# Moving the token sums of an up-projection from GpSimd to VectorE, asking later for two column sums, and moving one sum of a down-projection

## The chip, the cores and the metric

The kernel runs on one core of one Trainium2 chip. The metric is the device time of one execution in microseconds (us), as the median of several executions. A core has five engines with an instruction queue each: TensorE (PE, the matmuls), VectorE (DVE), ScalarE (ACT), GpSimd (POOL) and SyncE (SP), which here issues all the DMAs. Each engine takes the instructions of its queue in order; semaphores make an instruction wait for those of other engines.

## The reference, cut to what matters

One encoder block on 2048 tokens of width 1024, in float32: a mixer (a short convolution beside a gated linear attention), cross-attention into 256 memory rows, and a squared-ReLU MLP with a hidden width of 4096.

```python
def reference(x, mem, ...):
    for l in range(DEPTH):
        x = x + mixer_layer(x, ...)
        x = x + memory_cross_attention(x, mem, xa_norm[l], mem_norm[l], w_xq[l], w_xkv[l], w_xo[l])
        x = x + sq_relu_mlp(x, mlp_norm[l], w_up[l], w_down[l])
    return rms_norm(x, final_norm)

def sq_relu_mlp(x, mlp_norm, w_up, w_down):
    h = rms_norm(x, mlp_norm) @ w_up
    return jnp.square(jax.nn.relu(h)) @ w_down
```

The change touches the seam between the cross-attention and the MLP, the MLP's first product (up-projection) and its second (down-projection).

## The kernel before

**Precision and products.** Every float32 operand of a matmul is split into a high part (a cast on ACT, L113, in `split`) and a low part (a subtraction on DVE, L114), and a product is three matmuls: high by high, high by low, low by high (`mm3`, L141 to L143, or `product`, L1009). Activations lie transposed, features on the 128 partitions and tokens along the free axis.

**Order.** The program is written in Python, and a planner, which costs every instruction and orders each engine's queue by program order and by when it expects the operands, places the instructions. In the stretch of the change no engine's order is written by hand. A tile is taken from a ring of buffers with a fixed number (for instance seven `t2`, 28 `a`, eight `g`, two `st`, three `raw`, three `cv`, and four `ps` and four `pg` banks of PSUM) and given back when its last reader is done.

**Cross-attention.** It goes over eight blocks of 256 tokens (`s` = 0 to 7, L1028). For a block, `xa_probs` (L703) transposes the probabilities on PE (L712) and splits them, and `xa_out` (L717) multiplies them with the memory's values and adds the residual on DVE (L726). The last block uses `xa_last` (L729) instead: all eight PSUM banks are open at once, 192 matmuls run without a break, and eight additions on DVE (L741) empty them. After each block `sumsq` (L643) squares the result on ACT (L646, L648) and adds the squares up on DVE (L647, L649, L650, L651) to one 128x256 tile. `rstd_col` (L152) turns this tile into column sums by tiny matmuls with a vector of ones (L157), a scaling on DVE (L147) and a power on POOL (L149); `x2_rstd` (L654) stores the result in `rcol` (L657). In the last block `x2_rstd(s - 1)`, for block 6, stands between `xa_probs` and `xa_last`; block 7's own sum is asked for at L1063, before the loops of the up-projection, and stored at L1064. `x2_rows` (L659) spreads the values of `rcol` over the partitions, two blocks at a time. The values of blocks 6 and 7 are used first by `x2_rows` in the 13th step (`f == 12`) of the up-projection's first half.

**Up-projection.** It is a Strassen-like product with seven block products for eight. It runs over two halves of the tokens (`hf`, L1066) and in each over 16 steps (`f`, L1070). A step uses seven weight operands, made anew for each step by `weight_side` (L982) from `w_up`, and seven token operands, made once for each half by `token_side` (L960). Four 512-token by 512-feature quarters of the activations, loaded from `x2d` and scaled in `quarter` (L956, on DVE), are combined by `both` (L943): four calls in each half, for a22 + a21, that minus a11, a11 - a21, and a12 minus the second sum. Each call is two instructions of 128x1024. In the kernel before they run on POOL, through the helper `add` (L924). `operand` (L930) splits each result for the matmuls. The operands are used in the order 1, 4, 5, 6, 2, 7, 3. One step is 84 matmuls of 512 columns. ACT and DVE empty the banks: DVE's additions (L924) and squares (L1018), ACT's L1013, L1014 and L1084. The results go to `zu` in DRAM.

**Down-projection.** The same seven products over four groups of hidden features (`GROUPS`, of 4, 4, 3 and 3 blocks of 128), with the tokens in two parts, c = 0 and 1. `token_operands` (L1126) loads pieces of `zu` and combines them. `combine` (L1139) takes POOL unless it is told otherwise. It is called for s = u21 + u22 (POOL), for s - u11 (POOL), for a12 - s (DVE) and for a11 - a21 (POOL). `weight_operands` (L1162) does the like for the weights, on POOL. The matmuls are L1240, and DVE adds each bank into an accumulator (L924, `a<-ps,a` and `a<-pg,a`).

Of the kernel before, what the change touches and what calls it, by code (L numbers as in the profile page):

```python
# [30 lines left out]
def block_kernel(ctx, tc, x, mem, wm, wv, wlg, wlog, wout, wxk, wxv, wxqT, wxo, wup, wdn,  # L31
# [891 lines left out]
    def add(out, a, b, op=ALU.add, eng=nc.vector):  # L923
        eng.tensor_tensor(out=out, in0=a, in1=b, op=op)  # L924
# [17 lines left out]

    def both(out, a, b, op):  # L943
        for i in range(2):
            add(out[i], a[i], b[i], op, nc.gpsimd)

    def quarter(hf, b, k, t):

# [79 lines left out]
    for s in range(NS):  # L1028
        if s + 1 < NS:
            xa_scores(s + 1, 0, 0)  # L1030
            if s > 0:
                xa_probs(s, 0)
            xa_scores(s + 1, 0, 1)
            if s > 0:
                xa_probs(s, 1)
                x2_rstd(s - 1)
            xa_scores(s + 1, 1, 0)
            xa_scores(s + 1, 1, 1)
            if s == 0:
                xa_probs(s, 0)  # L1040
                xa_probs(s, 1)
        else:
            xa_probs(s, 0)
            xa_probs(s, 1)
            x2_rstd(s - 1)
            sides = [token_side(0)]
            next(sides[0])
            X = dict([next(sides[0])])
            W = weight_side(0, T2)
            X.update([next(sides[0])])  # L1050
            xa_last(s)
            f_last = sumsq(live[s]["xs"])
            continue
        xa_out(s, 0)
        if s + 2 < NS:
            xa_in(s + 2)
        if s in (4, 5):
            x2_rows(s - 4, s - 4)
        xa_out(s, 1)
        live[s]["f2"] = sumsq(live[s]["xs"])  # L1060
        if s + 2 < NS:
            xa_rstd(s + 2)
    r7 = rstd_col(f_last, PG)  # L1063
    nc.vector.tensor_copy(rcol[:, 14:16], r7)  # L1064

    for hf in range(2):  # L1066
        b0, b1 = 2 * hf, 2 * hf + 1
        if hf == 1:
            X = {}
        for f in range(16):  # L1070
            def x(i):
                if i not in X:
                    k, X[k] = next(sides[hf])
                    assert k == i
                return X[i]
            if f + 1 < 16:
                nxt = weight_side(f + 1)
            if hf == 0 and f == 14:
                sides.append(token_side(1))
                next(sides[1])  # L1080
            px, py, pz, pw = PS(), PG(), PS(), PG()
            product(px, W[1], x(1), True)
            c1 = T2()
            nc.scalar.copy(c1, px)  # L1084
            product(pw, W[4], x(4), True)
            product(pz, W[5], x(5), True)
            product(py, W[6], x(6), True)
            u2 = T2()
            add(u2, py, c1)
            product(px, W[2], x(2), False)  # L1090
            c11 = T2()
            sq_relu(c11, px, f, b0)
            product(py, W[7], x(7), False)
            add(c1, py, c1)
            c22 = T2()
            add(c22, pz, c1)
            sq_relu(c22, c22, f + 16, b1)
            add(c1, c1, pw, ALU.subtract)
            sq_relu_v(c1, f, b1)
            product(pz, W[3], x(3), False)  # L1100
            add(u2, pz, u2)
            sq_relu_v(u2, f + 16, b0)
            if hf == 0 and f == 12:
                for i in range(2):
                    x2_rows(2 + i, i)
            if hf == 0 and f == 15:
                nxt = weight_side(0)
            W = nxt
# [17 lines left out]
    def token_operands(c, fa, fb, n):  # L1126

        b0, b1 = 2 * c, 2 * c + 1

        def parts(src):  # L1130
            res = []
            for t in src:
                m = t.shape[1]
                hi, lo = (A4(F32R, (P, 2, TB))[:, :m] for _ in range(2))
                split(t, hi, lo)
                res += [(hi[:, j], lo[:, j]) for j in range(m)]
            return res

        def combine(out, a, b, op, eng=nc.gpsimd):  # L1139
            for o, x, y in zip(out, a, b):  # L1140
                add(o, x, y, op, eng)

        yield parts(raw_u(fa, n, b0))
        yield parts(raw_u(fb, n, b0))
        s = ST(F32, (P, 4, TB))
        s = [s[:, i:min(i + 2, n)] for i in range(0, n, 2)]
        for i, t in zip(range(0, n, 2), s):
            m = t.shape[1]
            nc.sync.dma_start(t, zu[(fa + i) * P:(fa + i + m) * P, b1 * TB:(b1 + 1) * TB].rearrange("(j p) t -> p j t", p=P))
        combine(s, s, raw_u(fb, n, b1), ALU.add)  # L1150
        yield parts(s)
        combine(s, s, raw_u(fa, n, b0), SUB)
        a12 = raw_u(fb, n, b0)
        combine(a12, a12, s, SUB, nc.vector)
        yield parts(a12)
        yield parts(s)
        yield parts(raw_u(fb, n, b1))
        a11 = raw_u(fa, n, b0)
        combine(a11, a11, raw_u(fa, n, b1), SUB)
        yield parts(a11)  # L1160
# [230 lines left out]
```

## Time and profile before

| | |
|---|---|
| median of 3 executions | 2741.66 us (2735.44 to 2743.51) |
| the profiled execution | 2743.17 us, with a span of 2741.3 us from its first to its last instruction |
| cross-attention's last block, from its transposes to the first up matmul | 1397.76 to 1431.16 us of the span |
| up-projection | 1431.16 to about 2078 us, its second half's matmuls from 1756.56 us |
| down-projection in seven products | about 2078 to 2610 us |

The page of the profile gives the share of each engine first, then the span in slices, the DMA queues, the chain of work that ended last, the costliest groups of instructions and the DMA issues. A row of the timeline reads: start, duration, engine, line, operation, output<-inputs, size, count, and in brackets how long the engine had sat idle and what ended it. Rows of one kind that follow each other are merged, with their count at the end. Several 128x1024 rows merged as x2 take twice the time of one.

### The profile page before, as it was taken

What the parts mean: (1) busy time and instruction counts of PE and PEld (TensorE: products, weight loads), DVE (VectorE), ACT (ScalarE), POOL (GpSimd) and SP (SyncE); (2) the same over time, 40 slices, a digit from 0 to 9 for tenths busy, and PEclk for the clock granted to TensorE, in tenths of its full rate; (3) what the DMA queues carried; (4) which work ended last, traced back from release to release, by engine and by line L of the source; (5) the groups of instructions that cost most, each with busy time, mean ns of one, the idle gap of its engine ahead of it and who ended that gap; (6) DMA issues with size and microseconds to landing.
All of it is one profiled execution on the core that took longest, in us unless ns stands there. A gap on an engine that the chain in (4) does not pass through costs nothing.

```text
span 2741.3 us, 34734 instructions
## 1 busy us (share of the span) xinstructions
PE 2611.3 (95%) x13560; PEld 2224.7 (81%) x13560; DVE 1632.1 (60%) x2430; ACT 933.6 (34%) x1432; POOL 396.7 (14%) x250
## 2 busy tenths in 40 slices
PE   7999989989889999999998999899999999999998
PEld 6898878877677787989886888688887788878877
DVE  6412363467757455343467557765655767788975
ACT  5411153423435443232234333433333222222322
POOL 1000010112210000000021000300002425243323
PEclk9999999999899999999999999999999999999999
DMA  7512355223444452101134332343338664545233
GB/s 246 180 61 68 100 175 167 77 89 116 129 122 157 150 184 85 62 31 47 47 119 151 104 119 96 112 139 115 113 117 301 203 200 143 178 160 183 94 104 112
DMA packets 198308, 353.26 MB, mean 129 GB/s; under 512 B 17344, under 2 KB 73792, under 8 KB 198144
## 3 DMA queue, kind: packets, MB, share of 16 engines
q1 hardware_dynamic: 198144, 351.05, 39.7%
q8 instruction: 106, 1.74, 0.3%
q14 instruction: 58, 0.48, 0.1%
HBM read 262.90 MB, written 88.08 MB: 128 GB/s over the span
## 4 chain that ended last, share of the span: by engine, by line
PE 76%; DVE 9%; DMA 5%; issue 4%; ACT 3%; POOL 2%; SPq 0%; POOLq 0%; DVEq 0%; ACTq 0%
PE ps L1009 12%; PE ps L141 9%; PE ps L142 9%; PE ps L143 9%; PE pg L1009 9%; PE pg L1240 8%; PE ps L1240 8%; PE pg L141 3%; PE pg L143 3%; PE pg L142 3%; DVE a L114 2%; DMA gt<-zv 1%; DVE g L114 1%; DMA raw<-zy 1%; DVE g L396 1%
## 5 line engine op out<-in xcount | busy, mean ns | idle before, releaser
L141 PE MATMUL ps<-a,a 128*128 128x512 f32 (+1 forms) x840 | 306.8, 365 | 6.8 <-DVE t L245 6.8
L142 PE MATMUL ps<-a,a 128*128 128x512 f32 (+1 forms) x840 | 306.2, 364 | 0.0
L143 PE MATMUL ps<-a,a 128*128 128x512 f32 (+1 forms) x840 | 306.1, 364 | 0.0
L1009 PE MATMUL pg<-a,g 128*128 128x512 f32 x1152 | 287.3, 395 | 13.1 <-DVE t L924 6.1
L1240 PE MATMUL pg<-a,g 128*128 128x512 f32 x1176 | 288.5, 392 | 10.4 <-DVE a L924 7.9
L1240 PE MATMUL ps<-a,g 128*128 128x512 f32 x1176 | 285.4, 389 | 1.7 <-DVE a L924 1.7
L1009 PE MATMUL ps<-a,g 128*128 128x512 f32 x1152 | 277.5, 389 | 0.2 <-ACT a L113 0.2
L1240 PEld LDWEIGHTS pg<-a,g 128*128 128x128 f32 x1176 | 222.6, 190 | 58.1 <-issue 8.9
L1009 PEld LDWEIGHTS pg<-a,g 128*128 128x128 f32 x1152 | 219.4, 191 | 61.5 <-DVE t L924 6.6
L1240 PEld LDWEIGHTS ps<-a,g 128*128 128x128 f32 x1176 | 220.7, 188 | 48.0 <-DVE a L924 2.1
L1009 PEld LDWEIGHTS ps<-a,g 128*128 128x128 f32 x1152 | 216.0, 188 | 45.4 <-ACT a L113 0.6
L113 ACT CAST a<-raw 128x1024 fp32r<-128x1024 f32 (+1 forms) x126 | 127.7, 1021 | 363.4 <-PE ps L1240 122.0
L114 DVE TENSOR_TENSOR a<-raw,a 128x1024 fp32r<-128x1024 f32 (+1 forms) x126 | 158.5, 1264 | 119.8 <-ACT a L113 118.0
L113 ACT CAST g<-gt 128x512 fp32r<-128x512 f32 x180 | 103.6, 618 | 342.9 <-PE pg L1009 203.8
L141 PEld LDWEIGHTS ps<-a,a 128*128 128x128 f32 x840 | 162.3, 193 | 32.4 <-DVE t L245 4.8
L143 PEld LDWEIGHTS ps<-a,a 128*128 128x128 f32 x840 | 162.7, 194 | 23.2
L142 PEld LDWEIGHTS ps<-a,a 128*128 128x128 f32 x840 | 162.5, 193 | 23.4 <-issue 0.2
L149 POOL TENSOR_TENSOR sm<-sm,nhalf 128x2 f32<-128x2 f32 (+1 forms) x26 | 23.0, 886 | 924.0 <-DVE sm L147 924.0
L114 DVE TENSOR_TENSOR g<-gt,g 128x512 fp32r<-128x512 f32 x180 | 142.5, 830 | 8.4 <-ACT g L113 8.3
L924 DVE TENSOR_TENSOR t<-pg,t 128x512 f32<-128x512 f32 x64 | 44.0, 688 | 172.6 <-PE pg L1009 170.7
L924 POOL TENSOR_TENSOR gt<-gt,t 128x512 f32<-128x512 f32 x42 | 65.7, 1581 | 459.7 <-DMA t<-in_wdn 390.1
L114 DVE TENSOR_TENSOR g<-raw,g 128x1024 fp32r<-128x1024 f32 (+3 forms) x90 | 103.3, 1158 | 33.0 <-ACT g L113 31.6
(327 smaller groups left out, 5380.8 us busy)
## 6 DMA issues: line engine op xcount, KB each, us to landing
zu<-t SPq DMA_DIRECT2D x128, 256.0 KB, 3.2
raw<-zu SPq DMA_DIRECT2D x64, 512.0 KB, 3.9
t<-in_wdn SPq DMA_DIRECT2D x84, 256.0 KB, 3.5
raw<-in_wm SPq DMA_DIRECT2D x32, 512.0 KB, 3.8
raw<-in_wup SPq DMA_DIRECT2D x32, 512.0 KB, 3.5
cv<-in_wup SPq DMA_DIRECT2D x32, 512.0 KB, 4.3
cv<-zu SPq DMA_DIRECT2D x32, 512.0 KB, 5.0
cv<-zu SPq DMA_DIRECT2D x40, 256.0 KB, 4.1
```

The costliest lines, as they stand in the source:

```text
L113: mark["act"] = nc.scalar.copy(hi, src)
L114: nc.vector.tensor_tensor(out=lo, in0=src, in1=hi.bitcast(F32), op=ALU.subtract)
L141: nc.tensor.matmul(ps, lh, rh, start=first, stop=False)
L142: nc.tensor.matmul(ps, lh, rl, start=False, stop=False)
L143: mark["pe"] = nc.tensor.matmul(ps, ll, rh, start=False, stop=last)
L149: nc.gpsimd.tensor_tensor(out=r, in0=v, in1=nhalf[:, :n], op=ALU.pow)
L396: nc.vector.tensor_tensor_scan(out=Q[hf][:, sl], data0=reset, data1=K[hf][:, sl], initial=0.0, op0=ALU.mult, op1=ALU.add)
L924: eng.tensor_tensor(out=out, in0=a, in1=b, op=op)
L1009: nc.tensor.matmul(ps, W[w][:, ks], X[x][kt], start=first and kt + w + x == 0, stop=kt == 3 and w == 1, skip_group_check=not first)
L1240: nc.tensor.matmul(ps, l, r, start=not chained and k == 0 and l is wh and r is x[k][0], stop=k == n - 1 and l is wl, skip_group_check=chained)
```

## The change

Five edits, in one diff. The sums of `both` go to `add`'s default engine, VectorE. `x2_rstd(6)` moves from ahead of `xa_last(7)` to behind it. The column sum of block 7 moves from ahead of the up-projection into its first step, behind the second of the seven products, and goes through `x2_rstd` too. In the down-projection the difference s - u11 is made on VectorE instead of GpSimd.

```diff
     def both(out, a, b, op):
         for i in range(2):
-            add(out[i], a[i], b[i], op, nc.gpsimd)
+            add(out[i], a[i], b[i], op)
...
             xa_probs(s, 0)
             xa_probs(s, 1)
-            x2_rstd(s - 1)
             sides = [token_side(0)]
             next(sides[0])
             X = dict([next(sides[0])])
             W = weight_side(0, T2)
             X.update([next(sides[0])])
             xa_last(s)
+            x2_rstd(s - 1)
             f_last = sumsq(live[s]["xs"])
             continue
...
-    r7 = rstd_col(f_last, PG)
-    nc.vector.tensor_copy(rcol[:, 14:16], r7)
-
     for hf in range(2):
...
             product(pw, W[4], x(4), True)
+            if hf == 0 and f == 0:
+                x2_rstd(NS - 1, f_last)
             product(pz, W[5], x(5), True)
...
         combine(s, s, raw_u(fb, n, b1), ALU.add)
         yield parts(s)
-        combine(s, s, raw_u(fa, n, b0), SUB)
+        combine(s, s, raw_u(fa, n, b0), SUB, nc.vector)
         a12 = raw_u(fb, n, b0)
         combine(a12, a12, s, SUB, nc.vector)
```

## The prediction

> **What bounds the kernel now.** I read the page's shares first, then busy time by stretch, then the timelines of PE, DVE and POOL where PE loses time.
>
> ```profile
> PE 2611.3 (95%) x13560; PEld 2224.7 (81%) x13560; DVE 1632.1 (60%) x2430; ACT 933.6 (34%) x1432; POOL 396.7 (14%) x250
> ...
> 1803.15 2.88 PE L1009 MATMUL pg<-a,g 128*128 128x512 f32 x12
> ...
> 1390.00:1431.00 41.00, 35.59 (x278) 34.97 (x277) 26.92 (x39) 9.92 (x18) 12.36 (x5) 0.92 0.24 78
> 1431.00:1482.00 51.00, 43.02 (x178) 33.09 (x177) 47.45 (x57) 24.88 (x33) 13.80 (x5) 0.97 0.53 181
> 1482.00:1732.00 250.00, 250.00 (x1107) 205.26 (x1105) 153.98 (x233) 90.88 (x146) 0.00 (x0) 1.00 0.35 110
> 1732.00:1790.00 58.00, 45.45 (x172) 35.96 (x171) 48.06 (x49) 26.39 (x36) 24.18 (x8) 0.85 0.42 125
> 2120.00:2200.00 80.00, 74.78 (x323) 61.45 (x323) 62.50 (x63) 22.85 (x30) 39.28 (x19) 0.98 0.60 196
> 2400.00:2500.00 100.00, 97.34 (x424) 80.24 (x423) 81.47 (x93) 28.23 (x42) 42.74 (x24) 0.98 0.53 167
> 2500.00:2610.00 110.00, 110.00 (x487) 90.99 (x486) 98.03 (x119) 28.86 (x42) 40.61 (x21) 1.00 0.37 122
> ```
>
> A stretch's row holds: length, then busy time and instruction count of PE, weight load, DVE, ACT and POOL, then the granted PE clock, DMA share and GB/s. PE is the bound. From 1482 to 1732 it never stops: 1107 matmuls, nearly all of 512 columns, take 250 us, 0.226 us each, so that there is nothing to gain. Elsewhere a stretch's loss is its length less its count times 0.226 (a little more in the first row, whose matmuls are half as wide). From 1431 to 1482 it is 51 - 178 x 0.226 = 10.8 us, from 1732 to 1790 58 - 38.9 = 19.1 us, in the two down rows up to 2500 7.0 and 4.2 us, after 2500 none. In both up stretches DVE is nearly full too (47.45 of 51, 48.06 of 58), and POOL, idle in the steady part, runs. These are the change's places.
>
> **Why DVE is full there.** Its rows grow when POOL works:
>
> ```profile
> 1391.54 1.22 DVE L114 TENSOR_TENSOR a<-raw,a 128x1024 fp32r<-128x1024 f32 x1
> 1396.26 3.41 DVE L114 TENSOR_TENSOR g<-raw,g 128x1024 fp32r<-128x1024 f32 x1
> ...
> L114 DVE TENSOR_TENSOR a<-st,a 128x1024 fp32r<-128x1024 f32 x8 | 11.9, 1495 | 0.0
> L114 DVE TENSOR_TENSOR g<-gt,g 128x512 fp32r<-128x512 f32 x8 | 11.1, 1422 | 0.0
> L114 DVE TENSOR_TENSOR a<-raw,a 128x1024 fp32r<-128x1024 f32 x3 | 4.9, 1627 | 3.4 <-ACT a L113 3.4
> L114 DVE TENSOR_TENSOR a<-cv,a 128x1024 fp32r<-128x1024 f32 x3 | 4.8, 1613 | 3.4 <-ACT a L113 3.3
> ...
> L114 DVE TENSOR_TENSOR g<-gt,g 128x512 fp32r<-128x512 f32 x44 | 28.4, 688 | 0.0
> ...
> 2146.72 1.21 DVE L924 TENSOR_TENSOR raw<-raw,st 128x1024 f32<-128x1024 f32 x1
> ```
>
> The same 128x1024 subtraction takes 1.22 us at 1391.54, with POOL idle, and 3.41 us at 1396.26, under a POOL sum. The four groups behind it are those of 1732 to 1790; the x44 row is from the steady part. Fourteen `a` splits take 21.6 us where 14 x 1.22 = 17.1 would do, eight `g` splits 11.1 where 8 x 0.688 = 5.5 would: 10.1 us of DVE time lost while POOL runs. A sum made on DVE costs 1.21 us (last row), so the eight of `both` in this half cost 9.7. DVE's load therefore stays the same; what goes is the detour over POOL.
>
> The Trainium skill, page "SBUF — State Buffer", section "Who interferes with whom", says that VectorE instructions with two SBUF inputs and GpSimd reads of SBUF exclude each other for a whole instruction, and that the earlier issue wins. By that rule the sum in this stretch would be the same 10.1 us, but a SUB moved to DVE would still be held up by what stays on POOL, which bears on the down part below.
>
> **The change, part by part.**
>
> A. *Cross-attention's last block.*
>
> ```profile
> 1393.01 3.32 DVE L114 TENSOR_TENSOR a<-cv,a 128x1024 fp32r<-128x1024 f32 x1
> 1402.70 2.50 DVE L650 TENSOR_TENSOR t<-t,a 128x512 f32<-128x512 f32 x1
> 1405.79 1.41 DVE L114 TENSOR_TENSOR gt<-pg,gt 128x256 fp32r<-128x256 f32 x4
> ...
> 1406.01 0.98 PE L157 MATMUL pg<-vec,t 128*128 128x1 f32 x4 [3.20 <-DVE t L651]
> ```
>
> The moved `x2_rstd(6)` takes its L157 (0.98 us, after a wait of 3.20), L147, a POOL power and a small copy behind the 192 matmuls; it issues no DMA, and its result is wanted only at `f == 12`. By itself this frees little: the next matmuls need the low part written by the first of the four splits at 1405.79, ready at about 1406.1. Those splits come late because DVE lost 2.1 us at 1393.01, 2.2 at 1396.26 and 1.9 at 1402.70 (0.6 alone), 6.2 in all, against 4 x 1.21 = 4.8 of new sums, which stand behind the splits in program order. A shorter gap may also save the half clock after 1406 (granted 0.92 in this stretch). Bounds 0 (one sum of 1.21 that comes ahead of the splits takes back what the L157 frees) to 6 us (its 3.20, and 2.8 from an earlier start of the splits and from the clock); I take 3.5, the middle, because neither DVE's order nor the clock is certain.
>
> B. *The up-projection's first step.*
>
> ```profile
> 1444.03 0.61 PE L157 MATMUL pg<-vec,t 128*128 128x1 f32 x4 [4.04 <-DVE t L651]
> 1444.50 7.33 PE L1009 MATMUL pg<-a,g 128*128 128x512 f32 x24
> ...
> 1459.43 1.65 PE L1009 MATMUL pg<-a,g 128*128 128x512 f32 x6 [1.37 <-DVE a L114]
> 1462.76 1.88 PE L1009 MATMUL pg<-a,g 128*128 128x512 f32 x7 [1.67 <-DVE a L114]
> ...
> 1439.78 2.72 DVE L650 TENSOR_TENSOR t<-t,a 128x512 f32<-128x512 f32 x1
> 1453.67 10.17 DVE L114 TENSOR_TENSOR a<-st,a 128x1024 fp32r<-128x1024 f32 x5
> ```
>
> Block 7's sum holds PE 4.04 us, and the 24 matmuls behind it take 7.33 instead of 24 x 0.226 + 0.2 = 5.6: 5.7 us in all. Its tile is late in part because L650 takes 2.72 us under POOL, where 0.6 would do. Two more waits, 1.37 and 1.67, end with splits that ran at 2 us each in the row of 10.17. The new place puts two products ahead of the sum, but before already had 36 matmuls ahead of it, so the planner may leave it where it is; then about half of the 4.04 stays. DVE gets 4 x 1.21 = 4.8 us of sums here and sheds 6 (2.1 on L650, 10.17 - 5 x 1.22 = 4.1 on the five splits). Bounds 2 (only DVE's relief, partly used) to 9 us (all of the waits); I take 5.5, nearest to the row of the 4.04 and its slow matmuls.
>
> C. *From the first half to the second.*
>
> ```profile
> 1752.24 4.48 PE L1009 MATMUL pg<-a,g 128*128 128x512 f32 x12 [6.14 <-DVE t L924]
> 1763.09 5.49 PE L1009 MATMUL ps<-a,gt 128*128 128x512 f32 x12 [2.96 <-DVE t L924]
> 1782.98 4.46 PE L1009 MATMUL pg<-a,g 128*128 128x512 f32 x12 [3.44 <-ACT a L113]
> ...
> 1749.19 2.40 DVE L114 TENSOR_TENSOR a<-cv,a 128x1024 fp32r<-128x1024 f32 x1 [3.31 <-ACT a L113]
> 1751.51 0.68 DVE L924 TENSOR_TENSOR t<-pg,t 128x512 f32<-128x512 f32 x1
> ```
>
> PE waits three times, 12.5 us, and runs its next twelve matmuls in 4.5 to 5.5 us, not 2.9, for 5.7 more. At 1752.24 it waits for the addition at 1751.51, which stands on DVE behind a split that waits for a POOL sum. That queue goes: both idle times of 3.4 us (the groups above) fall away, 6.8 us, as DVE's load is unchanged. DVE remains the bound: 48 of 58 us. So I take 7. Bounds 3 (half of the idle time comes back as other waits) to 11 us (the three waits less a leftover of 1.5).
>
> D. *The down-projection.* Sixteen differences leave POOL, twelve of 128x1024 and four of 128x512.
>
> ```profile
> L924 DVE TENSOR_TENSOR raw<-raw,st 128x1024 f32<-128x1024 f32 x8 | 16.7, 2091 | 13.0 <-POOL st L924 13.0
> L924 POOL TENSOR_TENSOR st<-st,raw 128x1024 f32<-128x1024 f32 x16 | 41.2, 2578 | 76.0 <-DMA raw<-zu 64.3 <-DVE a L114 10.6 <-DMA t<-in_wdn 1.2
> ...
> 2141.06 4.58 PE L1240 MATMUL pg<-a,g 128*128 128x512 f32 x12 [5.22 <-DVE a L924]
> 2438.63 3.63 PE L1240 MATMUL pg<-a,g 128*128 128x512 f32 x9 [2.66 <-DVE a L924]
> ...
> 2430.26 2.30 DVE L924 TENSOR_TENSOR raw<-raw,st 128x1024 f32<-128x1024 f32 x1 [3.56 <-POOL st L924]
> ```
>
> PE's long waits there are 5.22 and 2.66 us; with the slow rows behind them (4.58 for 2.88, 3.63 for nine) the two stretches lose 11.2. DVE stands still in front of the sum that follows the moved difference (3.56 us at 2430.26, 13.0 in the group's eight), and the additions that empty the banks queue behind it. Made on DVE, the difference is ready in order: no POOL wait. The new wait is for the `zu` piece, which the POOL rows show too. The price on DVE is 1.21 to 2.09 us, what the same kind of sum takes there on average, as much POOL work stays: 12 x 2.09 + 4 x 0.7 = 28 us, over 530 us in which DVE is idle for more than 100, less some relief. Bounds 0 (the DVE time is missed elsewhere, in the last group above all, 98.03 of 110) to 11; I take 7, nearest to the POOL waits that go.
>
> The clock's part depends on how long a leftover wait is. By the Trainium skill, page "TensorE: Matmul & The Clock Gate", section "What's actually happening", an idle window of about 3.4 us drops the clock, so that shorter leftover waits would cost only themselves; here the wait of 2.66 at 2438.63 was followed by a slow row, so the trace doesn't bear that out. With it D would be about 1.5 us better.
>
> **Sum.** 3.5 + 5.5 + 7 + 7 = 23 us less than the profiled 2743.17, or 2720. That execution was 1.5 us above the median of 2741.66, so against the median I forecast 2719, 0.8% faster.
>
> **The rivals.**
>
> 1. *DVE stays full and the sums take back the relief.* If the growth of DVE's rows isn't POOL's doing, 4.8 more on 47.45 of 51 and 9.7 more on 48.06 of 58 leave nothing in B and C. A would give 2 and D 7: 2733. Against it: 1.22 and 3.41 us for one operation.
>
> 2. *The column sum stays where it is.* The planner places block 7's L157 after 36 matmuls again. Then 2 us of wait and a part of the clock remain: 4 less, 2723.
>
> 3. *Slower: late `zu` pieces in front of DVE.* The difference on DVE waits for its load with the additions queued behind it. PE has four more banks, 4 x 2.72 = 10.9 us, so it decides from there on. POOL's waits for `zu` come to 64.3 us (the group above), among them these:
>
> ```profile
> 2267.11 2.42 POOL L924 TENSOR_TENSOR st<-st,raw 128x1024 f32<-128x1024 f32 x1 [15.41 <-DMA raw<-zu]
> 2421.93 2.52 POOL L924 TENSOR_TENSOR st<-st,raw 128x1024 f32<-128x1024 f32 x1 [5.39 <-DMA raw<-zu]
> ```
>
> At 15.4 in one side of each group, it costs 4 x (15.4 - 10.9 + 1.7 of clock) = 25, against 16 gained in A to C: 2751. Against it: the long wait stands before a first sum, which stays on POOL; before a moved difference, at 2421.93, it is 5.39.
>
> 4. *Everything goes*: the upper bounds, 6 + 9 + 11 + 11 = 37, or 2705.
>
> **How the numbers follow.** Forecast 0.60, with 2708 to 2731 as its own range; rival 1 0.15, rival 2 0.15, rival 3 0.05, rival 4 0.05. The lower bounds, 0 + 2 + 3 + 0 = 5, give 2737; less than 0 in D is rival 3. Range 2705 to 2737. A measurement of this kernel can tell about 0.3%, 8 us, from no change. Faster than 2733: 0.57 of the forecast, half of rival 1, rivals 2 and 4: 0.84. Slower: rival 3 and a little for the unforeseen, 0.06. Same: the rest, 0.10.
>
> **What would show it.** Right: no POOL instruction from 1390 to 1790 but small powers; DVE's 128x1024 splits at 1.2 us there; loss by count and pitch below 7 us at the first step and near 12 at the second half's; no L157 wait of 4 us on PE; in the down part no DVE wait for POOL `st`. Wrong: splits still of 2 to 3 us without POOL, new waits of PE for DVE's additions after 2078, or DVE waiting for `raw<-zu` for more than 11 us.

## The result, and the profile after

| | before | after |
|---|---|---|
| median (lowest to highest), 4 executions each | 2742.59 us (2735.44 to 2744.08) | 2706.61 us (2704.2 to 2709.59) |
| profiled execution, its span | 2743.17 us, 2741.3 us | 2705.29 us, 2703.5 us |

The ratio is 0.9873, with an interval of 0.9856 to 0.989: 1.3% faster, 36 us by the medians. The forecast was 2719 us, 23 us faster, with a range of 2705 to 2737. The direction is right and the time lies inside the range, but near its lower end: it is below the 2708 to 2731 that belong to the forecast's own sum, and close to the 2705 of the rival "everything goes".

To find the place of the gain, the span is cut at five points that both programs pass: the first transposes of cross-attention's last block, the first up matmul, the last of the row sums in the up-projection's 13th step (L165 of `x2_rows`), the last up matmul, and the start of the last matmul of the down-projection's seven products. "Tail" is what follows it.

| stage, us of the span | before | after | difference | predicted |
|---|---|---|---|---|
| ahead of the last block | 1397.8 | 1393.3 | -4.4 | 0 |
| last block of cross-attention (A) | 33.4 | 27.6 | -5.8 | -3.5 |
| first half up to the 13th step (B) | 259.9 | 251.5 | -8.4 | -5.5 |
| from there over the change of halves (C) | 387.1 | 370.4 | -16.7 | -7 |
| down-projection, seven products (D) | 549.4 | 544.7 | -4.7 | -7 |
| tail | 113.7 | 116.0 | +2.3 | 0 |

The 4.4 us in the first row lie ahead of every edited matmul and are no part of the change: in all fourteen kernels of this document the same 7744 matmuls lie there in the same order, and in their profiled executions they end anywhere from 1391.4 to 1397.8 us. The changed places give 33.3 us.

The shares at the head of the page after the change:

```profile
PE 2598.5 (96%) x13560; PEld 2213.8 (82%) x13560; DVE 1628.3 (60%) x2462; ACT 934.2 (35%) x1432; POOL 320.6 (12%) x218
```

POOL has 32 instructions and 76 us less. DVE has 32 instructions more and is busy 3.8 us *less* (1632.1 before): what it was given is paid for by what it no longer loses beside POOL. By stretches, with the columns of the prediction's rows (length; busy time and count of PE, weight load, DVE, ACT, POOL; granted PE clock; DMA share; GB/s), the places that answer to those rows:

```profile
1386.00:1421.00 35.00, 33.31 (x276) 32.70 (x274) 25.02 (x42) 9.88 (x19) 0.00 (x0) 1.00 0.28 91
1421.00:1463.00 42.00, 40.26 (x175) 31.74 (x175) 40.27 (x58) 23.37 (x32) 2.24 (x2) 1.00 0.65 216
1463.00:1713.00 250.00, 250.00 (x1106) 205.16 (x1105) 156.43 (x235) 91.86 (x147) 0.00 (x0) 1.00 0.35 110
1713.00:1771.00 58.00, 56.48 (x247) 45.47 (x246) 55.97 (x72) 32.41 (x46) 0.00 (x0) 1.00 0.48 150
2084.00:2164.00 80.00, 76.19 (x330) 62.58 (x329) 63.58 (x65) 22.74 (x30) 28.64 (x15) 0.98 0.60 196
2364.00:2464.00 100.00, 99.19 (x438) 81.87 (x437) 86.40 (x103) 28.54 (x43) 38.24 (x20) 1.00 0.56 179
2464.00:2574.00 110.00, 110.00 (x487) 91.06 (x487) 92.53 (x115) 28.67 (x42) 36.94 (x17) 1.00 0.38 119
```

PE's loss is again length less count times 0.226. At the first step it is 42 - 39.6 = 2.4 us (10.8 before), at the change of halves 58 - 55.8 = 2.2 us (19.1 before): 247 matmuls run in a stretch that held 172. In the two down rows 5.4 and 1.0 us remain (7.0 and 4.2). The granted clock is 1.00 where it was 0.92, 0.97 and 0.85. POOL runs only two small powers in the first four rows.

The waits that are left in the timeline of PE, with the two column sums (a bracket holds the idle time ahead of a row and what ended it):

```profile
1398.03 0.38 PE L142 MATMUL pg<-gt,a 128*128 128x256 f32 x1 [1.15 <-DVE gt L114]
...
1420.55 0.50 PE L157 MATMUL pg<-vec,t 128*128 128x1 f32 x4
...
1430.12 0.50 PE L157 MATMUL pg<-vec,t 128*128 128x1 f32 x4
...
1747.60 2.56 PE L1009 MATMUL pg<-a,g 128*128 128x512 f32 x10 [0.65 <-DVE g L114]
1751.32 1.66 PE L1009 MATMUL ps<-a,g 128*128 128x512 f32 x6 [0.88 <-DVE a L114]
...
2105.34 4.34 PE L1239 MATMUL pg<-a,g 128*128 128x512 f32 x12 [3.81 <-DVE a L924]
```

Neither column sum waits. At the change of halves three waits of 12.5 us in all have become two of 1.5. One long wait is left, in the down-projection's first group.

**The change of halves, with equal work.** The row sizes of the stretches differ, so here is one piece of work in both kernels, 254 matmuls from the first half's 15th step into the second half. By stretch, before:

```profile
1732.45:1808.82 76.37, 63.82 (x254) 51.16 (x253) 62.16 (x70) 32.76 (x47) 24.18 (x8) 0.89 0.40 124
```

After:

```profile
1713.75:1773.64 59.89, 58.37 (x254) 47.17 (x254) 57.54 (x74) 33.27 (x47) 0.00 (x0) 1.00 0.50 153
```

16.5 us shorter. DVE's groups in it (count | busy us, mean ns of one | idle time ahead and what ended it), before:

```profile
L114 DVE TENSOR_TENSOR g<-gt,g 128x512 fp32r<-128x512 f32 x12 | 13.7, 1178 | 0.0
L114 DVE TENSOR_TENSOR a<-st,a 128x1024 fp32r<-128x1024 f32 x8 | 11.9, 1495 | 0.0
L114 DVE TENSOR_TENSOR a<-raw,a 128x1024 fp32r<-128x1024 f32 x3 | 4.9, 1627 | 3.4 <-ACT a L113 3.4
L114 DVE TENSOR_TENSOR a<-cv,a 128x1024 fp32r<-128x1024 f32 x3 | 4.8, 1613 | 3.4 <-ACT a L113 3.3
...
L924 DVE TENSOR_TENSOR t<-ps,t 128x512 f32<-128x512 f32 x6 | 4.1, 687 | 2.0 <-PE ps L1009 2.0
L924 DVE TENSOR_TENSOR t<-pg,t 128x512 f32<-128x512 f32 x6 | 4.1, 684 | 5.3 <-PE pg L1009 5.3
```

After:

```profile
L114 DVE TENSOR_TENSOR a<-st,a 128x1024 fp32r<-128x1024 f32 x8 | 9.6, 1221 | 0.0
L114 DVE TENSOR_TENSOR g<-gt,g 128x512 fp32r<-128x512 f32 x12 | 7.7, 688 | 0.0
L924 DVE TENSOR_TENSOR t<-pg,t 128x512 f32<-128x512 f32 x6 | 4.1, 690 | 0.3 <-PE pg L1009 0.3
...
L114 DVE TENSOR_TENSOR a<-cv,a 128x1024 fp32r<-128x1024 f32 x3 | 3.7, 1223 | 0.1
L114 DVE TENSOR_TENSOR a<-raw,a 128x1024 fp32r<-128x1024 f32 x3 | 3.7, 1221 | 0.0
```

The splits are back at 1.22 and 0.69 us: four groups took 13.7 + 11.9 + 4.9 + 4.8 = 35.3 us and take 24.7, 10.6 less. Against this stand eight new sums, 8 x 1.22 = 9.8 us. DVE's own load thus fell by only 0.8 us for this work; most of the rest of the 4.6 us (62.16 - 57.54) is four small DVE additions, 2.7 us, that now fall outside the stretch. The large change is in DVE's idle time, 76.37 - 62.16 = 14.2 us before and 59.89 - 57.54 = 2.3 after. Of the 14.2, 6.7 waited for ACT's casts behind POOL's sums, and 7.3 waited for PE to fill a bank, while PE waited for DVE at other moments.

### The profile page after: what moved, and what is told of

It reads as the page before. It is cut to its first block, busy times and chain, and to the rows that moved or that the text cites. A ratio compares the mean times of both kernels' runs of the same rounds, so it can differ in the third digit from the quotient of the medians.

```text
span 2703.5 us, 34725 instructions
## 1 busy us (share of the span) xinstructions
PE 2598.5 (96%) x13560; PEld 2213.8 (82%) x13560; DVE 1628.3 (60%) x2462; ACT 934.2 (35%) x1432; POOL 320.6 (12%) x218
## 4 chain that ended last, share of the span: by engine, by line
PE 60%; DVE 6%; DMA 4%; issue 2%; ACT 2%; POOL 1%; SPq 0%; POOLq 0%; DVEq 0%; ACTq 0%
PE ps L1009 12%; PE pg L1239 9%; PE pg L1009 9%; PE ps L1239 9%; PE ps L141 4%; PE ps L143 4%; PE ps L142 4%; PE pg L143 3%; PE pg L141 2%; PE pg L142 2%; DVE a L114 1%; DMA gt<-zv 1%; DVE g L114 1%; DMA raw<-zy 1%; DMA raw<-zA 1%
## 5 line engine op out<-in xcount | busy, mean ns | idle before, releaser
L924 POOL TENSOR_TENSOR gt<-gt,t 128x512 f32<-128x512 f32 x42 | 75.4, 1810 | 806.8 <-DMA t<-in_wdn 729.0
L114 DVE TENSOR_TENSOR g<-gt,g 128x512 fp32r<-128x512 f32 x180 | 134.0, 783 | 9.5 <-ACT g L113 9.3
L924 DVE TENSOR_TENSOR a<-pg,a 128x512 f32<-128x512 f32 (+1 forms) x128 | 84.2, 669 | 65.6 <-PE pg L1239 47.4
```

Of the source, the lines that this page charges most:

```text
L114: nc.vector.tensor_tensor(out=lo, in0=src, in1=hi.bitcast(F32), op=ALU.subtract)
```

## The experiments

The stages of all runs, in us of the profiled execution's span (A to D as above; the medians stand with each run). The runs were measured in three sessions, in which the median of the kernel before was 2739.18, 2741.21 and 2740.71 us, against 2742.59 beside the kernel after. Where a run is compared with the kernel after by medians, a difference of 3 us or less therefore tells nothing.

| kernel | A | B | C | D | tail | span |
|---|---|---|---|---|---|---|
| before | 33.4 | 259.9 | 387.1 | 549.4 | 113.7 | 2741.3 |
| after | 27.6 | 251.5 | 370.4 | 544.7 | 116.0 | 2703.5 |
| e1, sums of `both` alone | 30.6 | 251.0 | 370.5 | 552.5 | 113.7 | 2715.7 |
| e2, column sums alone | 33.5 | 261.0 | 385.4 | 549.6 | 114.0 | 2740.0 |
| e3, down difference alone | 34.1 | 260.7 | 387.3 | 543.2 | 113.5 | 2733.1 |
| e4, `both` in the second half alone | 32.8 | 259.9 | 370.5 | 551.2 | 114.8 | 2724.1 |
| e6, after without the down difference | 29.0 | 251.5 | 370.4 | 550.5 | 114.5 | 2710.0 |
| e8, after without the move of block 6's sum | 29.0 | 250.6 | 370.4 | 543.8 | 115.4 | 2706.3 |
| e5, after with large POOL load | 27.6 | 266.2 | 381.3 | 544.7 | 113.5 | 2730.0 |
| e9, after with POOL load as before | 27.6 | 263.3 | 380.1 | 545.1 | 113.9 | 2723.6 |
| e10, after with a detour over POOL | 29.0 | 256.6 | 378.5 | 544.3 | 113.5 | 2715.2 |
| e7, after with one more down sum on DVE | 29.0 | 251.5 | 370.4 | 538.4 | 115.2 | 2696.1 |
| e11, all down token sums on DVE | 27.6 | 251.5 | 370.6 | 537.0 | 109.8 | 2687.9 |
| e12, the weight sums too | 27.5 | 251.5 | 370.5 | 536.3 | 109.5 | 2688.8 |

A stage of PE is long for two reasons: PE stands idle, or its granted clock is halved. The profiles tell the two apart (PE idle is the stage's length less PE's busy time; half clock is the time at a granted clock of 0.50), and in A and D this matters:

| kernel | A | PE idle | half clock | D | PE idle | half clock |
|---|---|---|---|---|---|---|
| before | 33.4 | 5.4 | 6.8 | 549.4 | 12.1 | 6.8 |
| after | 27.6 | 1.7 | 0 | 544.7 | 7.2 | 6.8 |
| e1 | 30.6 | 1.8 | 6.8 | 552.5 | 12.0 | 13.7 |
| e3 | 34.1 | 4.9 | 10.2 | 543.2 | 7.6 | 3.4 |
| e4 | 32.8 | 5.4 | 3.4 | 551.2 | 12.0 | 13.7 |
| e6 | 29.0 | 1.7 | 3.4 | 550.5 | 10.9 | 13.7 |
| e8 | 29.0 | 1.8 | 3.4 | 543.8 | 6.8 | 6.8 |
| e7 | 29.0 | 1.7 | 3.4 | 538.4 | 3.1 | 3.4 |
| e11 | 27.6 | 1.7 | 0 | 537.0 | 3.4 | 0 |

The idle time follows the edits. The half clock does so only in part: with the same waits in A (0.37 and 1.15 us), it lasts 3.4 us in e6, e7 and e10 and does not come in the kernel after, e5, e9, e11 and e12. The last section says what it depends on.

### Each edit alone

**e1.** The kernel before, with one edit.

```diff
-            add(out[i], a[i], b[i], op, nc.gpsimd)
+            add(out[i], a[i], b[i], op)
```

> The kernel before with one edit: the sums of the up-projection on VectorE, everything else as before. Between equal PE work the changed kernel gained 5.8 us up to the first up matmul, 8.4 us from there to the spreading of the row sums in the 13th step, 16.8 us over the change of halves and 2.3 us behind it (after 4.4 us that lie ahead of all edits). If the sums' place carries the seam too: 24 us or more in all, with the change of halves at 16 to 17 and the two places ahead of it at 7 to 11 of their 14. If the two column sums carry the seam: 17 to 19 us, the change of halves alone, and PE still waits about 4 us at the column sum of block 7.

Measured: 2712.66 us against 2739.18, ratio 0.9907 (0.9893 to 0.992), 26.5 us faster. It has B and C of the kernel after to within 0.5 us, and half of A. In A PE's idle time is that of the kernel after, too (1.8 against 1.7 us, 5.4 before); the 3 us between them go with 6.8 us at half clock.

**e2.** The kernel before, with the two column sums moved and nothing else.

```diff
-            x2_rstd(s - 1)
...
             xa_last(s)
+            x2_rstd(s - 1)
...
-    r7 = rstd_col(f_last, PG)
-    nc.vector.tensor_copy(rcol[:, 14:16], r7)
...
+            if hf == 0 and f == 0:
+                x2_rstd(NS - 1, f_last)
```

> The kernel before with only the two column sums asked for later. If the sums on GpSimd carry the seam: at most 5 us, since the low parts that the last block's matmuls need still come at the same time and the squares of block 7 are still added up at GpSimd's pace; the first step's loss goes from 10.8 to 6 or more. If the column sums carry it: 10 to 14 us. Change of halves as before, within 1 us, in both cases.

Measured: 2741.41 us against 2739.18, ratio 1.0008 (0.9998 to 1.0017): nothing. The timeline of PE in e2:

```profile
1405.00 0.58 PE L142 MATMUL pg<-gt,a 128*128 128x256 f32 x1 [2.98 <-DVE gt L114]
...
1438.74 2.37 PE L1009 MATMUL ps<-a,g 128*128 128x512 f32 x9 [1.47 <-DVE a L114]
1443.01 0.61 PE L157 MATMUL pg<-vec,t 128*128 128x1 f32 x4 [1.91 <-DVE t L651]
```

And of DVE, just ahead of the last row:

```profile
1435.27 3.42 DVE L114 TENSOR_TENSOR a<-cv,a 128x1024 fp32r<-128x1024 f32 x1
...
1439.21 3.41 DVE L114 TENSOR_TENSOR a<-raw,a 128x1024 fp32r<-128x1024 f32 x1
```

In the last block the wait of 3.20 us at the column sum is now one of 2.98 at the next matmul, which needs a split that is as late as before. At the first step the column sum waits for 1.91 us in place of 4.04, but the stage is no shorter: the splits of 3.4 us that delay the sum's tile delay the operands too, and the matmuls ahead of the column sum now wait 1.47 us for one. The wait was where the lateness showed, not where it came from.

**e3.** The kernel before, with the down difference on DVE.

```diff
-        combine(s, s, raw_u(fa, n, b0), SUB)
+        combine(s, s, raw_u(fa, n, b0), SUB, nc.vector)
```

> The kernel before with only the down-projection's difference on VectorE. By my prediction 7 us (0 to 11); by the comparison of the two traces 2 to 5, since the profiled down-projection of the changed kernel is only 4.7 us shorter and its tail gives 2.3 back. If late pieces of zu in front of VectorE cost something, slower than before.

Measured: 2737.32 us against 2739.18, ratio 0.9986 (0.9976 to 0.9996): about 2 us by the medians, 4 by the ratio. The profiled stage D is 6.2 us shorter. PE's waits in it:

```profile
2138.37 4.58 PE L1240 MATMUL pg<-a,g 128*128 128x512 f32 x12 [4.29 <-DVE a L924]
2432.01 2.29 PE L1240 MATMUL pg<-a,g 128*128 128x512 f32 x9 [0.70 <-DVE a L924]
```

The second wait went from 2.66 to 0.70 us, and its nine matmuls are at full speed (2.29, not 3.63): 3.3 us. The first, 5.22 before, lost only 0.9. Of the 6.2 us, 4.5 are idle time of PE (12.1 to 7.6); the rest goes with 3.4 us less at half clock.

**e4.** The kernel before, with the sums of `both` on DVE in the second half alone.

```diff
-    def both(out, a, b, op):
+    def both(out, a, b, op, eng):
         for i in range(2):
-            add(out[i], a[i], b[i], op, nc.gpsimd)
+            add(out[i], a[i], b[i], op, eng)
...
-        s = a22
-        both(s, a21, a22, ALU.add)
+        s, eng = a22, nc.vector if hf else nc.gpsimd
+        both(s, a21, a22, ALU.add, eng)
...
```

(and so for the other three calls of `both`)

> The kernel before with the sums on VectorE in the second half of the tokens alone. If the change of halves stands by itself: 16 to 17 us, all of it between the 13th step of the first half and the 3rd of the second, and nothing ahead of it. If part of it came from an order that the planner changed further ahead: under 12 us.

Measured: 2725.84 us against 2739.18, ratio 0.9946 (0.9933 to 0.996). C is 16.6 us shorter, A and B are as before: the eight sums of the second half do all of C, and those of the first half all that e1 gains in A and B.

### Parts taken back from the kernel after

**e6.** The kernel after, with the difference s - u11 on POOL again (e3's edit undone).

> The changed kernel with the down-projection's difference back on GpSimd. By the single edit's run (3.8 us of 2739): 2 to 6 us slower than the changed kernel, with a wait of about 5 us for VectorE's additions early in the first group and one of 2 to 3 in the third. If the edit does nothing next to the others: within 1 us.

Measured: 2711.73 us, ratio to before 0.9892 (0.9879 to 0.9906): 5.1 us slower than the kernel after. D is 5.8 longer: PE is idle for 3.7 us more in it, and the rest goes with 6.8 us more at half clock.

**e8.** The kernel after, with `x2_rstd(s - 1)` ahead of `xa_last` again.

> The changed kernel with block 6's column sum back ahead of the last block's matmuls. With the sums of the up-projection on VectorE and the column sums as before, the stretch from the last block's transposes to the first up matmul was 30.5 us, with both it was 27.6. If that difference is this step's: 2 to 3 us slower than the changed kernel, with a wait of 1.4 us at the column sum and a slower clock behind it. If it is the planner's order of VectorE: within 1 us.

Measured: 2707.04 us, ratio 0.9869 (0.9852 to 0.9885), the same as the kernel after. Moving block 6's column sum is worth nothing in company either. Stage A reads 27.6 to 30.6 us in all kernels with the sums of the first half on DVE, and 29.0 both with block 6's sum moved (e6) and with it left (e8): the rest is how long PE's half clock lasts after the wait ahead of the 192 matmuls. It costs 1.4 us for 3.4 us of it (e8, e6) and 3.0 for 6.8 (e1), and with the same edits it comes in one kernel and not in another.

### What POOL took: DVE's speed, or the order

Two theories can explain e1. By the first, POOL's sums slow down DVE's instructions. By the second, what counts is that ACT and DVE wait for POOL's results. The next three kernels put the one or the other back into the kernel after.

**e5.** POOL sums that nobody reads, beside the splits, so that DVE is slowed but no one waits. This adds 64 sums of 256 columns to the work; the outputs don't use them.

```diff
-    def operand(src):
+    def operand(src, extra=False):
...
+            for j in range(4 if extra else 0):
+                sl = slice(j * 256, (j + 1) * 256)
+                add(reset, c[i][:, sl].bitcast(F32), c[2 + i][:, sl].bitcast(F32), eng=nc.gpsimd)
...
-        yield 5, operand(s)
+        yield 5, operand(s, True)
...
```

(and so for the operands 6, 7 and 3)

> The changed kernel with extra sums on GpSimd whose results nobody uses: for operands 5, 6, 7 and 3 of each half, each of the two high parts plus its low part, in four pieces of 256 columns, into a table that is no longer needed. At the 0.74 us that a sum of 256 columns took on GpSimd before, that is 24 us of GpSimd for each half, as much as the sums that left it (24.2 at the change of halves). No engine waits for them. If the loss of before came from the detour (VectorE and ScalarE waiting for GpSimd's results): at most 5 us slower than the changed kernel. If it came from VectorE's instructions being stretched while GpSimd works: most of the 16.6 us of the change of halves and part of the 8 to 9 of the first step come back, 12 us or more, with splits of 2 to 3.4 us.

Measured: 2728.3 us against 2741.21, ratio 0.9958 (0.9944 to 0.9971): 21.7 us slower than the kernel after. Here the expected sign did not come: the 128x1024 `a` splits of C stay at 1.21 us, and it is other DVE instructions that grow, the `g` splits from 687 to 830 ns on average and the squares from 688 to 819. The dose was larger than meant, 39.5 us of POOL in each half against 24 in the kernel before, so it was repeated.

**e9.** The same with 32 sums of 384 columns.

```diff
+            for j in range(2 if extra else 0):
+                sl = slice(j * 384, (j + 1) * 384)
+                add(cst[:, 128:512], c[i][:, sl].bitcast(F32), c[2 + i][:, sl].bitcast(F32), eng=nc.gpsimd)
```

> The same test as the extra sums on GpSimd that nobody waits for, with the dose matched: two pieces of 384 columns for each of the eight tiles of a half, estimated from the 1.6 us that 128x512 took on GpSimd at 1.2 to 1.6 us each, 20 to 25 us of GpSimd for each half against 24 before. The larger dose (39.5 us for each half) brought back 10.9 of 16.6 us at the change of halves and 14.7 in the first half. If stretching alone made the loss of before: 16 to 17 at the change of halves. If it scales with GpSimd's time: about 6 to 7 there and 8 to 9 in the first half, so that the wait for GpSimd's results must carry the rest.

Measured: 2724.68 us against 2740.71, ratio 0.9942 (0.9928 to 0.9957): 18 us slower than the kernel after. POOL's group, and DVE's groups over 1715 to 1790 us in e9:

```profile
L924 POOL TENSOR_TENSOR cst<-a,a 128x384 f32<-128x384 f32 x32 | 54.7, 1711 | 305.6 <-DVE a L114 297.0 <-ACT t L1084 6.6
```

```profile
L114 DVE TENSOR_TENSOR g<-gt,g 128x512 fp32r<-128x512 f32 x15 | 11.5, 809 | 0.0
L114 DVE TENSOR_TENSOR a<-st,a 128x1024 fp32r<-128x1024 f32 x8 | 10.0, 1274 | 0.0
L1021 DVE SCALAR_TENSOR_TENSOR t<-t 128x512 f32<-128x512 f32 x6 | 6.6, 1098 | 0.0
```

Nobody waits for these sums, 27 us in each half, and yet C is 9.7 us longer than in the kernel after and B 11.8, which lies between the two cases of the expectation. Here too it is the squares (1098 ns, 688 without POOL) and the short splits that grow. That is more in B than the change gained there, because here all of the first half's load falls into B, while in the kernel before part of it lay in A.

**e10.** The reverse: the sums stay on DVE, and behind each comes a chain of six POOL multiplications of one column by ones. They leave every value as it is and load POOL little, but ACT must wait for the chain.

```diff
             add(out[i], a[i], b[i], op)
+            for _ in range(6):
+                add(out[i][:, 0:1], out[i][:, 0:1], onec, ALU.mult, nc.gpsimd)
```

> The changed kernel with the wait and without the load: behind each of VectorE's sums a chain of six GpSimd multiplications of one column by one, in place, so that the split must wait for GpSimd as before but GpSimd reads next to nothing. Estimated 1.5 to 4 us for a chain (a power of two columns took 0.7 to 1.1 us, a scaling of four 0.24). If the wait for GpSimd carries the rest of the loss: 6 to 10 us back at the change of halves, with VectorE's splits at 1.2 us. If waits of this length are hidden: under 3.

Measured: 2716.42 us against 2740.71, ratio 0.9915 (0.9898 to 0.9931): 9.8 us slower than the kernel after; B 5.1 and C 8.1 us longer. DVE's groups over 1722 to 1782 us, and one row of the waits over 1690 to 1800 us (total, times, longest):

```profile
L114 DVE TENSOR_TENSOR a<-st,a 128x1024 fp32r<-128x1024 f32 x7 | 8.4, 1220 | 1.9 <-ACT a L113 1.9
...
L114 DVE TENSOR_TENSOR a<-raw,a 128x1024 fp32r<-128x1024 f32 x3 | 3.7, 1221 | 2.5 <-ACT a L113 2.5
```

```profile
ACT a L113 <- POOL raw L924: 12.4, 2, 6.5
```

The splits are at full speed, and DVE waits for ACT, which waits for POOL, as in the kernel before. So both theories are true of a part. At the change of halves slower instructions alone give back 9.7 of the 16.7 us, and waiting alone 8.1; together 17.8, about all of it. That each costs a large part is shown; the shares are estimates. The doses are not those of the kernel before: in C of e10 ACT waits 16.9 us for POOL, 11.9 before, and in e9 other instructions grow than the `a` splits of before.

### The down-projection: what else was to be had

**e7.** The kernel after, with the first sum u21 + u22 on DVE too.

```diff
-        combine(s, s, raw_u(fb, n, b1), ALU.add)
+        combine(s, s, raw_u(fb, n, b1), ALU.add, nc.vector)
```

> The changed kernel with the down-projection's first sum on VectorE too. If the remaining wait of 3.8 us in the first group is the port's doing (sums of 3.4 us beside GpSimd): 3 to 5 us faster. If VectorE then stands in front of pieces of zu that come late (GpSimd waited 30.3 and 15.7 us for them): slower, by up to 4 x 5 us; PE bears about 10.9 us of such a wait.

Measured: 2698.37 us against 2741.21, ratio 0.9845 (0.9831 to 0.9858): 8.2 us faster than the kernel after. The wait that was left in the kernel after, at 2105.34, has its cause in DVE's timeline there:

```profile
2089.63 3.42 DVE L924 TENSOR_TENSOR st<-st,cv 128x1024 f32<-128x1024 f32 x1
2092.98 3.42 DVE L924 TENSOR_TENSOR raw<-raw,st 128x1024 f32<-128x1024 f32 x1
```

beside these of POOL, also in the kernel after:

```profile
2088.59 3.38 POOL L924 TENSOR_TENSOR st<-st,raw 128x1024 f32<-128x1024 f32 x1
2091.92 3.39 POOL L924 TENSOR_TENSOR st<-st,cv 128x1024 f32<-128x1024 f32 x1
```

They are the sums u21 + u22 that the change left on POOL. Without them, over the down-projection in e7, the wait of PE for DVE's additions and the longest waits of DVE for `zu` (total, times, longest) are:

```profile
PE pg L1239 <- DVE a L924: 1.1, 1, 1.1
```

```profile
DVE st L924 <- DMA raw<-zu: 3.2, 3, 1.4
```

3.81 us of wait have become 1.1, and PE's idle time in D went from 7.2 to 3.1 us. D is 6.3 us shorter, more than the 3 to 5 expected; 3.4 us less at half clock are in it. And the first sums of a piece, which on POOL waited up to 30.3 us for `zu` in the kernel after, wait at most 1.4 on DVE: in its queue they stand where the load has almost landed.

**e11.** e7, and a11 - a21 on DVE.

```diff
-        combine(a11, a11, raw_u(fa, n, b1), SUB)
+        combine(a11, a11, raw_u(fa, n, b1), SUB, nc.vector)
```

> The changed kernel with all sums of the down-projection's token side on VectorE (the first sum, which alone gave 8 us more, and the last difference, a11 - a21). If less GpSimd time is what helps: 0 to 4 us faster than with the first sum alone. If VectorE, 109 of 130 us busy in the third group then, becomes the bound: slower than with the first sum alone by 2 or more.

Measured: 2692.41 us against 2740.71, ratio 0.9826 (0.981 to 0.9842). This is the fastest of all, 14.2 us below the kernel after by the medians and 6.0 below e7, beyond the 0 to 4 expected. But the edit's own stage shows little of that: in D PE is idle for 3.4 us, 3.1 in e7, and D is 1.4 us shorter by its half clock. Most of the 6 us lie in the tail, 109.8 us against 115.2, whose own instructions the edit leaves as they are: PE's waits for the tail's first splits go from 1.85 and 1.84 us in e7 to at most 0.72. That the moved sums let DVE come to these splits earlier is likely, but was not tried.

**e12.** e11, and the 56 sums of the weights on DVE.

```diff
-                add(o, x, y, SUB, nc.gpsimd)
+                add(o, x, y, SUB)
```

> In addition all weight sums of the down-projection on VectorE, 42 + 14 of 128x512, 0.6 us each, 34 us more over four groups, so that GpSimd has nothing to do there. Relief by what is left of the stretching (GpSimd is still busy for 134 us there). If the stretching returns about what the sums cost: within 4 us of the run before. If VectorE becomes the bound: 10 us slower or more, in the last group first.

Measured: 2693.51 us, ratio 0.9832 (0.9815 to 0.9849), as e11. The last 120 us of the seven products in e11:

```profile
2460.00:2580.00 120.00, 120.00 (x531) 99.32 (x529) 104.34 (x142) 33.90 (x48) 13.24 (x9) 1.00 0.40 130
```

and in e12:

```profile
2460.00:2580.00 120.00, 120.00 (x532) 99.37 (x531) 105.79 (x151) 33.70 (x47) 0.00 (x0) 1.00 0.41 132
```

Nine sums more, some 6 us at 0.68 us each, add only 1.5 us to DVE's busy time: the rest is what DVE no longer loses beside POOL. PE never stops in either.

## Why the prediction was right, and where it was not

**The bound, right.** PE lost time where DVE was nearly full beside POOL, and its loss there, by count and pitch, is nearly gone. The signs named for a right forecast are there: only powers on POOL from 1386 to 1771, splits at 1.22 us, no L157 wait, no DVE wait for POOL's `st` in the down-projection. But "near 12 at the second half's" was to be the loss left there; it is 2.2 us.

**A, the mechanism right, the size at its upper bound.** 3.5 was forecast, 5.8 came. That moving L157 "frees little" by itself is shown by e2, and that the splits were late because of POOL by e1. PE's idle time fell by 3.7 us (5.4 to 1.7), near the forecast. The other 2.1 us are the clock, 6.8 us at half clock before and none after. That part is luck: with the same waits e6, e7 and e10 keep 3.4 us of half clock and an A of 29.0.

**B, 5.5 forecast, 8.4 measured: the step that failed is the choice of the price** "nearest to the row of the 4.04 and its slow matmuls". It took the column sum's wait for the cost and DVE's relief for a lesser part ("only DVE's relief, partly used", 2 us). The runs show the reverse: the move alone gives nothing (e2), and DVE's relief alone gives all of it (e1, B at 251.0). In the kernel after, the column sum stands behind 40 matmuls of the up-projection where 36 were before, nearly where it was, and does not wait.

**C, 7 forecast, 16.7 measured: the term that was mis-sized most.** The step was "6.8 us, as DVE's load is unchanged. DVE remains the bound: 48 of 58 us." That the load hardly changes was right (10.6 us of relief against 9.8 of sums). But an engine that is busy for 48 of 58 us is idle for 10, and only the part of it whose releaser led to POOL was counted. The other idle time, that in which DVE waited for PE (7.3 us before, 0.3 after), was left out. It was PE's own lateness come round: DVE late, PE stalls, the banks fill late, DVE stands idle, and its work piles up behind. With the delay gone, both kinds of idle time went (14.2 to 2.3 us), and with them PE's slow clock (granted 0.89 to 1.00). The upper bound of 11 was too low for another reason: it left out the 5.7 us of slow matmuls that the same part had just worked out. The three waits less the leftover of 1.5, with these 5.7, come to 12.5 - 1.5 + 5.7 = 16.7 us, which is what was measured. C should have been priced by what PE loses, and was priced by DVE's idle time. That the whole still fell inside the range is owed to the bounds of the other parts; C by itself lies outside its own.

That "what goes is the detour over POOL" was half of it. e9 and e10 show slower instructions and waiting at about equal weight, 9.7 and 8.1 us. The sum was right about DVE's busy time and yet missed this: it set the relief against the new sums, one for one, but at the end the new sums cost PE next to nothing (2.5 us of loss are left over the 254 matmuls), while DVE's lost time is dear to PE (in C of e9 DVE's groups grow by about 8 us, and the stage is 9.7 us longer). That this is so because a sum can be placed where DVE has room, and a slowed split cannot, is argued from this and was not tried.

**D, 7 forecast; 6.2 in the profile of e3, 5.1 by the medians of e6 and the kernel after, 2 to 4 by those of e3.** The mechanism is right: DVE's waits for POOL went, and the wait at 2438.63 with its slow rows. The size was taken too large: PE's idle time in D falls by 4.9 us (before to after), 4.5 (e3) and 3.7 (e6 to after), for the first wait, 5.22 us, went down only to 3.81, held up by the sums that stay on POOL. The price was less than thought: the twelve large differences take 20.6 us on DVE in the kernel after, not 25. Over stage D and the tail the whole change shows only 4.7 - 2.3 = 2.4 us, but the tail varies from 113.5 to 116.0 us between these kernels (e11 and e12 apart). Stage D was 2 to 3 us longer in e1 and e4, which move only the sums of `both`. PE's idle time there is that of before, 12.0 against 12.1 us, but it runs for 13.7 us at half clock, not 6.8: this is the clock again, and not the edit.

That "a SUB moved to DVE would still be held up by what stays on POOL", taken from the Trainium skill, page "SBUF — State Buffer", section "Who interferes with whom", came out: the moved difference took 3.42 us at 2089.63 beside POOL's 3.38, and e7 removed most of the wait by removing POOL's sums. On the clock, the one wait over 3.4 us that is left, 3.81 us, was followed by a slow row (4.34 us for twelve), as the section "What's actually happening" of the Trainium skill's page "TensorE: Matmul & The Clock Gate" has it. That shorter waits "would cost only themselves", which the prediction drew from it, the runs refute: in e8 a wait of 1.42 us was followed by 3.4 us at half clock.

**The rivals.** The first (the growth is not POOL's doing) fell with the kernel after, where all splits run at 1.22 us, and with e5 and e9, where POOL's load alone makes DVE's rows grow again. The second had its condition nearly fulfilled, since the column sum hardly moved, but not its price, since what made it late was gone. The third, late `zu` pieces, was to decide from 10.9 us on; in the kernel after DVE does not wait for `zu` at all, and in e7, where all first sums stand on DVE as well, no wait of theirs passes 1.4 us. The fourth came nearest, 37 us against 36, though not by its own terms: C went past its bound and D stayed below.

**The sum.** `both` alone gives 26.5 us (e1), the down difference 5.1 (e6), the column sums nothing that a run shows, together 31.6 of 36. The rest is within what profiles of the same code differ by, as the 4.4 us ahead of the change show; no run divides it further.

## What to carry to other kernels

Where two engines wait for each other in turns, price the change by what the bounding engine loses, its waits with the slow rows behind them (16.7 us here), and not by the idle time of the other one whose releaser is the engine that you unload (6.8). Before a waiting instruction is moved, ask why its input is late: if the same lateness reaches the next instruction, the move is worth nothing. And a sum handed to GpSimd is not free where VectorE is busy: here 27 us of unused GpSimd sums in a half cost 10 to 12 us, and giving VectorE the down-projection's first sum too made the kernel 8 us faster.

## What was unexpected of the hardware

**Small work on POOL is dear.** A sum of 384 columns took 1.71 us (e9), and a multiplication of a single column took 0.31 to 0.54 us on average, 18 to 31% of it. Two of POOL's groups in e10:

```profile
L924 POOL TENSOR_TENSOR raw<-raw,vec 128x1 f32<-128x1 f32 x24 | 12.9, 537 | 319.4 <-DVE raw L924 317.8
L924 POOL TENSOR_TENSOR cv<-cv,vec 128x1 f32<-128x1 f32 x24 | 7.4, 307 | 1.6
```

**Several short waits slow PE's clock as a long one does.** The tail of the kernel after, on PE:

```profile
2592.05 0.50 PE L142 MATMUL pg<-a,g 128*128 128x512 f32 x1 [1.88 <-DVE a L114]
2594.39 0.50 PE L143 MATMUL pg<-a,g 128*128 128x512 f32 x1 [1.83 <-DVE g L114]
2595.07 0.80 PE L141 MATMUL pg<-a,g 128*128 128x512 f32 x1 [0.19 <-ACT g L113]
2595.66 0.63 PE L142 MATMUL pg<-a,g 128*128 128x512 f32 x1
```

and the same place in e11:

```profile
2581.04 0.50 PE L143 MATMUL pg<-a,g 128*128 128x512 f32 x1 [0.72 <-DVE g L114]
2581.96 0.50 PE L141 MATMUL pg<-a,g 128*128 128x512 f32 x1 [0.41 <-ACT g L113]
2583.37 0.50 PE L143 MATMUL pg<-a,g 128*128 128x512 f32 x1 [0.68 <-DVE g L114]
2583.71 0.40 PE L141 MATMUL ps<-a,g 128*128 128x512 f32 x1
```

In the kernel after, two waits of 1.9 and 1.8 us, one matmul apart, are followed by rows of 0.63 where 0.39 to 0.40 is full speed; in e11 three waits that add up to 1.8 us are followed by full speed. The kernel after has 16.6 us at half clock in its tail, e11 9.7; with 2.9 us less of idle PE, this accounts for most of e11's shorter tail.

**Where the clock falls.** In the traces of all fourteen kernels every spell of half clock begins on a fixed grid of 3.413 us and lasts whole steps of it, where the end of the execution doesn't cut it. What counts is how busy PE was in the step before. From 1380 us on there are 5340 steps at full clock. All 70 in which PE was busy for less than 45% were followed by half clock, and none of the 5211 in which it was busy for more than 60%; of the 59 between, 14 were. So about 1.9 us of idle PE within one step are enough, in one wait or in several; from 1.4 us on it may happen. And the same wait costs the clock or not by where it falls on the grid. Since the grid's place against the stages changes from profile to profile, a difference of 1 to 3 us between two profiles of A or D can be this alone.
